# Order of a gate group's products, order of two readers of one PSUM bank, and a table lookup in 16 bits, in a two-layer encoder kernel

## The chip, the core and the metric

The kernel runs on one core of a Trainium2 chip. The metric is the time of one execution in microseconds on the device. TensorE does the matrix products (in the profile PE, its weight loads PEld), VectorE is DVE, ScalarE is ACT, GpSimd is POOL and SyncE, which issues most transfers, is SP. Each engine takes its instructions strictly in the order in which the program issues them, and waits on semaphores of the others.

## What is computed

A trunk of two layers on 256 tokens of width 1024. Each layer is an attention mixer and a PEER feed-forward part, and the change lies in the second:

```
def chunk(xc):
    q = (xc @ w_query).reshape(PEER_CHUNK, PEER_HEADS, 2, half)
    s = jnp.einsum('thpk,pnk->thpn', q, sub_keys)
    sv, si = lax.top_k(s, PEER_TOPK)
    cand = (sv[:, :, 0, :, None] + sv[:, :, 1, None, :]).reshape(...)
    cidx = (si[:, :, 0, :, None] * PEER_N_KEYS + si[:, :, 1, None, :]).reshape(...)
    top_s, sel = lax.top_k(cand, PEER_TOPK)
    eidx = jnp.take_along_axis(cidx, sel, axis=-1)
    g = jax.nn.softmax(top_s, axis=-1)
    u = expert_down[eidx]
    vv = expert_up[eidx]
    act = jax.nn.gelu(jnp.einsum('td,thkd->thk', xc, u), approximate=False)
    return jnp.einsum('thk,thkd->td', (g * act), vv)
```

For each token, 8 heads choose 16 of 128 x 128 experts each. Expert number is 128 i + j.

## The kernel before

The kernel does not gather the experts of `expert_down`. It multiplies all 16384 of them with all tokens, takes the gelu, and multiplies by a dense table of gates, which is zero where a token did not choose an expert. All products on TensorE take operands split in two (`wh`, `wl`, lines 189 and 192: ScalarE rounds the loaded tile, VectorE subtracts), so three products stand for one.

In one layer the stages of the feed-forward part follow each other so:

1. **Scores and choice** (lines 913 to 950): `score_lane`, `topk_lane`. VectorE finds the 16 best of each half and the 16 best sums.
2. **Numbers of the experts** (`index_lane`, lines 952 to 1003). A choice `sel` is a place in a 16 x 16 table. For its high and low four bits in turn, line 974 compares with 0 to 15 (2048 elements a partition), line 977 multiplies with the key numbers `sif`, and line 979 sums over the 16.
3. **Downs** (lines 1302 to 1304): 128 units a layer, each 24 products of 128x256, with two units to one PSUM bank `acc`. `gelu_lane` (lines 1234 to 1256) then has ScalarE take the gelu into `act`.
4. **Gate groups** (`gate_group`, lines 1011 to 1066), which run between the downs: 32 groups of 8 tokens for each of two halves of i, 64 a layer. For a group VectorE builds one-hot tables: `ej` of j, `ei` of i, and `ag`, which is `ei` times the gate, in two parts (high part `ag[:, 0]`, rest `ag[:, 1]`). ScalarE scales `ej` to `el` (line 1022). For each token t TensorE issues three small products: a count (`ei` with `ej`, line 1041), high gates (`ag[:, 0]` with `ej`) and low gates (`ag[:, 1]` with `el`, both line 1045). The result is a bank `b` of 8 tokens by 64 values of i.
5. **Where gate and gelu meet.** For an i whose gelu is there already (the first `g` of the 64), VectorE multiplies `act` by the gates from the bank (line 1059); for the others ScalarE copies the gates into `act` (line 1062), and `gelu_lane` multiplies later: it takes the gelu of tokens that have gates in place (line 1244), writes the gelu of the others to `act` (line 1249) and has VectorE multiply (line 1252). Where both engines read one bank, the second in program order waits for the first.
6. **Ups** (line 1336): the experts that any token chose, ranked, sent and read back, are multiplied by their gates, in products of 128x512.

What sets the order is a planner at build time (`Lanes`, from line 55). The main line emits TensorE's units; every side job is a generator, a lane, that asks for an engine with an estimated cost (`vcost`, `scost`) and is let in by a clock for each engine. The estimates decide between which units of the downs a group falls. Once emitted, the order is fixed, also that between engines. Four buffers of `wh` and `wl` let the splits run ahead, and two sets of one-hot tables and two banks let two groups overlap.

Of the kernel before, what the change touches and what calls it, by code (L numbers as in the profile page):

```python
# [12 lines left out]
F16 = mybir.dt.float16  # L13
# [42 lines left out]
def vcost(n):  # L56
    return 0.1 + n * 0.00105
# [157 lines left out]
def encoder_kernel(ctx, tc, x_in, wts, downs, ups, gains, gate_bias, qk_norm, rpb, sink, skeys, consts, sums, out,  # L215
                   depth=DEPTH):
    nc = tc.nc
# [79 lines left out]
    iota2 = cpool.tile([128, 128, 2], F16, name="iota2")  # L297
    tiny = cpool.tile([128, 2], F32, name="tiny")
# [16 lines left out]
    iota16 = cst[:, C_I16:C_I16 + 16]  # L315
# [146 lines left out]
    for l in range(depth):  # L462
# [5 lines left out]
        if l == 0:  # L468
# [23 lines left out]
            nc.vector.tensor_copy(iota2, cst[:, C_IOTA:C_IOTA + 128][:, :, None].to_broadcast([128, 128, 2]))  # L492
            acc_first = first_half(u, "T1")
# [371 lines left out]
        def area(off, n, u32=False):  # L865
            return (afu if u32 else afl)[:, A0 + off:A0 + off + n]
# [88 lines left out]
        def index_lane():  # L955
            yield from lane_need(["top"])
            for ch in range(2):
                w = lambda k: area(M2 + k * 128, 128).rearrange("p (h k) -> p h k", k=16)
                wu = lambda k: area(M2 + k * 128, 128, True).rearrange("p (h k) -> p h k", k=16)
                sif = area(M2 + 8 * 128, 256).rearrange("p (h q k) -> p h q k", q=2, k=16)  # L960
# [8 lines left out]
                nc.vector.tensor_copy(w(2), wu(1))  # L969
                nc.vector.tensor_copy(w(3), wu(7))  # L970
                for q in range(2):
                    eq = area(11264, 2048).rearrange("p (h k a) -> p h k a", h=8, a=16)
                    yield ("v", vcost(2048))
                    nc.vector.tensor_tensor(eq, w(2 + q)[:, :, :, None].to_broadcast([128, 8, 16, 16]),
                                            iota16[:, None, None, :].to_broadcast([128, 8, 16, 16]), op=OP.is_equal)
                    yield ("v", vcost(2048))
                    nc.vector.tensor_mul(eq, eq, sif[:, :, q, None, :].to_broadcast([128, 8, 16, 16]))
                    yield ("v", vcost(2048))
                    nc.vector.tensor_reduce(w(4 + q), eq, axis=AX.X, op=OP.add)
# [30 lines left out]
        def gate_group(r, n, o):  # L1010
# [29 lines left out]
            for t in range(8):  # L1040
                nc.tensor.matmul(cnts[r][:, half * w:(half + 1) * w], ej[:, t // 2, :, t % 2],
                                 ei[:, t // 2, i0 - p0:i0 - p0 + w, t % 2], start=counted[r] == 0 and t == 0,
                                 stop=counted[r] == NG - 1 and t == 7, skip_group_check=True)
                for k, e in enumerate((ej, el)):
                    nc.tensor.matmul(b[:, t * 64:(t + 1) * 64], e[:, t // 2, :, t % 2],
                                     ag[:, k, t // 2, :, t % 2], start=k == 0, stop=k == 1)
# [8 lines left out]
            g = min(max(2 * gelus[0] - p0, 0), 64)  # L1055
            if g:
                t = lanes.use("v", vcost(8 * g) - 0.35)
                a = act[:, p0:p0 + g, half, t0:t0 + 8]
                nc.vector.tensor_mul(a, a, bv[:, 0:g])
            if g < 64:  # L1060
                t = max(t, lanes.use("s", scost(8 * (64 - g)), lanes.cur - 0.3))
                nc.scalar.activation(act[:, p0 + g:p0 + 64, half, t0:t0 + 8], bv[:, g:64], AF.Copy)
# [172 lines left out]
        def gelu_lane(b, acc):  # L1235
# [9 lines left out]
            for c in range(2):  # L1245
                g0 = min(max(g - 128 * c, 0), 128)
                a, ac = act[:, 2 * b:2 * b + 2, c], av[:, :, 128 * c:128 * c + 128]
                if g0 < 128:
                    nc.scalar.activation(a[:, :, g0:128], ac[:, :, g0:128], AF.Gelu)  # L1249
                if g0:  # L1250
                    t = max(t, lanes.use("v", vcost(2 * g0), lanes.cur))
                    nc.vector.tensor_mul(a[:, :, 0:g0], a[:, :, 0:g0], ac[:, :, 0:g0])
# [255 lines left out]
```

## Time and profile before

| | |
|---|---|
| runs | 1885.28, 1888.07, 1889.13 us (median 1888.07) |
| profiled execution, its time | 1889.17 us |
| its span, first to last instruction | 1887.4 us |
| granted TensorE clock | 0.992 |
| PE busy | 1846.0 us, 98% |
| DVE busy | 1493.7 us, 79% |
| ACT busy | 1075.3 us, 57% |
| POOL busy | 423.9 us, 22% |

A matmul's busy time in the profile reaches to the end of its pipeline: a 128x256 product is shown as 282 ns, while the next one starts 120 ns later. So a busy PE can still lose time, and what it loses is read from the distances between starts. In the windows view a row gives the stretch, its length, then for each engine the busy time and in brackets the number of instructions, then granted clock, DMA share and GB/s. In the timeline a row gives start, duration, engine, line and operation, and in square brackets the idle time ahead of it with what ended it.

### The profile page before, as it was taken

How to read it: one execution, taken by the hardware profiler on the slowest of the kernel's cores; microseconds unless marked ns; L12 is line 12 of the kernel's file. 1: busy time of each engine (PE TensorE's matmuls, PEld its weight loads, DVE VectorE, ACT ScalarE, POOL GpSimd, SP SyncE). 2: the span in 40 equal slices, each digit the busy share in tenths (PEclk: the TensorE clock that was granted, in tenths of full speed). 3: DMA queues.
4: the chain of work that ended last, by engine and by line, in shares of the span. 5: the costliest groups of instructions: out<-in, count | busy, mean ns of one | idle time of the engine just before them, and what ended most of it. 6: DMA issues, size and time to landing. Idle time of an engine off the chain costs nothing. (4 is left out here: it accounts for less than half of the span.)

```text
span 1887.4 us, 37955 instructions
## 1 busy us (share of the span) xinstructions
PE 1846.0 (98%) x14826; PEld 1672.6 (89%) x14826; DVE 1493.7 (79%) x3017; ACT 1075.3 (57%) x1710; POOL 423.9 (22%) x374
## 2 busy tenths in 40 slices
PE   8999999999999999999899999999999999999998
PEld 7889899999999977888778989999999999778886
DVE  6976899888887797756689778999788877976565
ACT  4665544556556565645646654455566565666454
POOL 0000000000027456744200000000000374567341
PEclk8999999999999999999999999999999999999999
DMA  7435456554457688997464354555444587889873
GB/s 255 158 101 171 155 163 190 177 166 157 152 162 233 215 272 278 312 285 227 167 219 137 111 174 146 179 188 179 156 158 147 176 234 224 260 284 323 261 229 121
DMA packets 125139, 372.98 MB, mean 198 GB/s; under 512 B 16528, under 2 KB 38672, under 8 KB 124944
## 3 DMA queue, kind: packets, MB, share of 16 engines
q1 hardware_dynamic: 91440, 256.93, 44.2%
q0 software_dynamic: 33504, 113.47, 17.4%
q8 instruction: 120, 1.97, 0.4%
q14 instruction: 75, 0.61, 0.1%
HBM read 342.87 MB, written 27.47 MB: 196 GB/s over the span
## 5 line engine op out<-in xcount | busy, mean ns | idle before, releaser
L192 DVE TENSOR_TENSOR wl<-raw,wh 128x1024 fp32r<-128x1024 f32 x478 | 580.0, 1221 | 200.2 <-ACT wh L189 196.7
L189 ACT ACTIVATE wh<-raw 128x1024 fp32r<-128x1024 f32 x478 | 504.3, 1058 | 254.4 <-PE bank L1336 76.3
L1302 PE MATMUL bank<-TT,wh 128*128 128x256 f32 x2048 | 587.0, 287 | 0.0
L1303 PE MATMUL bank<-TT,wh 128*128 128x256 f32 x2048 | 577.2, 282 | 0.0
L1304 PE MATMUL bank<-TT,wl 128*128 128x256 f32 x2048 | 577.1, 282 | 0.0
L1336 PE MATMUL bank<-wh,TT 128*128 128x512 f32 x1416 | 397.9, 400 | 8.3 <-PEq L1351 5.9
L1302 PEld LDWEIGHTS bank<-TT,wh 128*128 128x128 f32 x2048 | 386.2, 189 | 0.3
L1303 PEld LDWEIGHTS bank<-TT,wh 128*128 128x128 f32 x2048 | 386.0, 188 | 0.0
L1304 PEld LDWEIGHTS bank<-TT,wl 128*128 128x128 f32 x2048 | 385.0, 188 | 0.0
L1336 PEld LDWEIGHTS bank<-wh,TT 128*128 128x128 f32 x1416 | 266.0, 189 | 75.0 <-issue 6.7
L1152 POOL DMA_INDIRECT rows<-act,rank x200 | 220.4, 1102 | 374.0 <-DVE miss L1124 313.6
L192 DVE TENSOR_TENSOR wl<-act,wh 128x1024 fp32r<-128x1024 f32 x132 | 161.4, 1224 | 93.1 <-ACT wh L189 87.9
L1336 PE MATMUL bank<-wl,TT 128*128 128x512 f32 x708 | 225.5, 398 | 0.0
L189 ACT ACTIVATE wh<-act 128x1024 fp32r<-128x1024 f32 x132 | 139.7, 1060 | 120.0 <-PE bank L1336 113.0
L870 POOL IOTA act<- 128x128 uint32 x4 | 1.8, 438 | 805.3 <-PE bank L355 417.5
L1249 ACT ACTIVATE act<-bank 128x256 f32<-128x256 f32 (+7 forms) x240 | 79.8, 369 | 173.1 <-PE bank L1304 121.5
L1336 PEld LDWEIGHTS bank<-wl,TT 128*128 128x128 f32 x708 | 134.1, 189 | 32.7
L1022 ACT ACTIVATE el<-ej 128x1024 f16<-128x1024 f16 x128 | 133.2, 1050 | 19.9 <-DVE ej L1019 19.3
L1211 POOL DMA_INDIRECT act<-in_ups_dram,act x96 | 117.3, 1222 | 101.4 <-DVE TT L1229 88.0
L435 PE MATMUL bank<-TT,wh 128*128 128x256 f32 x448 | 129.6, 289 | 1.5 <-ACT raw_ka L563 1.0
L437 PE MATMUL bank<-TT,wh 128*128 128x256 f32 x448 | 126.4, 282 | 0.0
L438 PE MATMUL bank<-TT,wl 128*128 128x256 f32 x448 | 126.3, 282 | 0.0
(252 smaller groups left out, 2969.9 us busy)
## 6 DMA issues: line engine op xcount, KB each, us to landing
raw<-in_downs_dram SPq DMA_DIRECT2D x256, 512.0 KB, 3.7
raw<-in_wts_dram SPq DMA_DIRECT2D x132, 512.0 KB, 3.9
act<-in_ups_dram SPq DMA_DIRECT2D x36, 512.0 KB, 5.9
act<-rows SPq DMA_DIRECT2D x82, 129.0 KB, 4.3
raw<-in_ups_dram SPq DMA_DIRECT2D x20, 512.0 KB, 5.7
act<-rows SPq DMA_DIRECT2D x84, 64.5 KB, 4.4
rows<-act,rank POOLq DMA_INDIRECT x200, 6.0
Sq<-in_rpb_dram SPq DMA_DIRECT2D x2, 876.0 KB
```

The costliest lines, as they stand in the source:

```text
L189: self.nc.scalar.activation(h, r, AF.Copy)
L192: self.splits.append(self.nc.vector.tensor_sub(lo, r, h.bitcast(F32)).ins.name)
L435: nc.tensor.matmul(o, wh, rh, start=first and i == 0 and pc == 0, stop=False, skip_group_check=True)
L437: nc.tensor.matmul(o, wh, rl, start=False, stop=False, skip_group_check=True)
L438: nc.tensor.matmul(o, wl, rh, start=False, stop=last and i == len(kcs) - 1 and pc == 1, skip_group_check=True)
L1022: nc.scalar.activation(el, ej, AF.Copy, scale=LOW)
L1152: snd = nc.gpsimd.indirect_dma_start(byrank[r], bass.IndirectOffsetOnAxis(ap=rank[:, i:i + 1], axis=0), afl[:, i * ROW:(i + 1) * ROW], None)
L1211: nc.gpsimd.indirect_dma_start(w, None, ups_rows, bass.IndirectOffsetOnAxis(ap=num, axis=0), element_offset=l * 16384 * D)
L1302: nc.tensor.matmul(o, lh, TT[:, :, 0, kc, :], start=kc == 0, stop=False)
L1303: nc.tensor.matmul(o, lh, TT[:, :, 1, kc, :], start=False, stop=False)
L1304: nc.tensor.matmul(o, ll, TT[:, :, 0, kc, :], start=False, stop=kc == 7)
L1336: nc.tensor.matmul(oacc[ch][hf], a, r[:, hf * 512:(hf + 1) * 512], start=first[hf] and a is lh and r is h, stop=last and a is ll)
```

## The change

It has four edits, and the planner lays out the whole order anew with them.

- **The group's products.** All counts and high gates of the 8 tokens come first, then the 8 low gates. The flag that starts a sum is now set once for the bank.
- **Two readers of a bank.** In `gate_group` ScalarE's copy of the late i is emitted ahead of VectorE's multiplication; in `gelu_lane` ScalarE writes the gelu for both halves first, and VectorE multiplies behind.
- **The lookup.** The table of 0 to 15, the numbers and the compared bits are float16 (the numbers are under 128). The sum over 16 is four halvings by additions.
- **The planner's figures** for these steps follow.

```
+    i16 = cpool.tile([128, 8, 2], F16, name="i16")
...
+            nc.vector.tensor_copy(i16.rearrange("p a s -> p (a s)"), cst[:, C_I16:C_I16 + 16])
...
-                nc.vector.tensor_copy(w(2), wu(1))
-                nc.vector.tensor_copy(w(3), wu(7))
+                for k in range(2):
+                    nc.vector.tensor_copy(wh(2 + k), area(M2 + (1, 7)[k] * 128, 128, True)[:, :, None].to_broadcast(
+                        [128, 128, 2]))
...
-                    yield ("v", vcost(2048))
-                    nc.vector.tensor_tensor(eq, w(2 + q)[:, :, :, None].to_broadcast([128, 8, 16, 16]),
-                                            iota16[:, None, None, :].to_broadcast([128, 8, 16, 16]), op=OP.is_equal)
-                    yield ("v", vcost(2048))
-                    nc.vector.tensor_mul(eq, eq, sif[:, :, q, None, :].to_broadcast([128, 8, 16, 16]))
-                    yield ("v", vcost(2048))
-                    nc.vector.tensor_reduce(w(4 + q), eq, axis=AX.X, op=OP.add)
+                    yield ("v", vcost(1024) + 0.3)
+                    nc.vector.tensor_tensor(eq, wh(2 + q)[:, :, None, :].to_broadcast([128, 128, 8, 2]),
+                                            i16[:, None, :, :].to_broadcast([128, 128, 8, 2]), op=OP.is_equal)
+                    yield ("v", vcost(1024))
+                    nc.vector.tensor_mul(e4, e4, sif[:, :, q, None, :].to_broadcast([128, 8, 16, 16]))
+                    for m in (8, 4, 2, 1):
+                        yield ("v", vcost((64 if m > 1 else 128) * m))
+                        nc.vector.tensor_add(w(4 + q)[:, :, :, None] if m == 1 else e4[:, :, :, 0:m], e4[:, :, :, 0:m],
+                                             e4[:, :, :, m:2 * m])
...
-                for k, e in enumerate((ej, el)):
-                    nc.tensor.matmul(b[:, t * 64:(t + 1) * 64], e[:, t // 2, :, t % 2],
-                                     ag[:, k, t // 2, :, t % 2], start=k == 0, stop=k == 1)
+                nc.tensor.matmul(b[:, t * 64:(t + 1) * 64], ej[:, t // 2, :, t % 2],
+                                 ag[:, 0, t // 2, :, t % 2], start=t == 0, stop=False, skip_group_check=True)
+            for t in range(8):
+                nc.tensor.matmul(b[:, t * 64:(t + 1) * 64], el[:, t // 2, :, t % 2],
+                                 ag[:, 1, t // 2, :, t % 2], start=False, stop=t == 7, skip_group_check=True)
...
+            if g < 64:
+                t = lanes.use("s", scost(8 * (64 - g)), lanes.cur - 0.5)
+                nc.scalar.activation(act[:, p0 + g:p0 + 64, half, t0:t0 + 8], bv[:, g:64], AF.Copy)
             if g:
-                t = lanes.use("v", vcost(8 * g) - 0.35)
+                t = lanes.use("v", vcost(8 * g) - 0.35, t if g < 64 else 0.0)
                 a = act[:, p0:p0 + g, half, t0:t0 + 8]
                 nc.vector.tensor_mul(a, a, bv[:, 0:g])
-            if g < 64:
-                t = max(t, lanes.use("s", scost(8 * (64 - g)), lanes.cur - 0.3))
-                nc.scalar.activation(act[:, p0 + g:p0 + 64, half, t0:t0 + 8], bv[:, g:64], AF.Copy)
...
             for c in range(2):
-                g0 = min(max(g - 128 * c, 0), 128)
-                a, ac = act[:, 2 * b:2 * b + 2, c], av[:, :, 128 * c:128 * c + 128]
+                g0 = max(g - 128 * c, 0)
                 if g0 < 128:
-                    nc.scalar.activation(a[:, :, g0:128], ac[:, :, g0:128], AF.Gelu)
-                if g0:
-                    t = max(t, lanes.use("v", vcost(2 * g0), lanes.cur))
-                    nc.vector.tensor_mul(a[:, :, 0:g0], a[:, :, 0:g0], ac[:, :, 0:g0])
+                    nc.scalar.activation(act[:, 2 * b:2 * b + 2, c, g0:128], av[:, :, 128 * c + g0:128 * c + 128],
+                                         AF.Gelu)
+            if g:
+                t = lanes.use("v", vcost(2 * g), t)
+                for c in range(1 + (g > 128)):
+                    a = act[:, 2 * b:2 * b + 2, c, 0:min(g - 128 * c, 128)]
+                    nc.vector.tensor_mul(a, a, av[:, :, 128 * c:min(g, 128 * c + 128)])
```

What this does to the fixed order is seen at two places. The first is TensorE's queue at the start of a gate group late in the first layer's downs (`ej1`, `el1`, `ag1` are the group's one-hot tables, `bank4` its gates, `bank7` the counts). Before:

```order
L1041 LDWEIGHTS ej1_2241 [waits DVE_49]
L1041 MATMUL bank7_7004<-ei1_2245,ej1_2241 128x36 [waits DVE_49]
L1045 LDWEIGHTS ej1_2241 [waits DVE_49]
L1045 MATMUL bank4_8745<-ag1_2247,ej1_2241 128x64 [waits PE_49]
L1045 LDWEIGHTS el1_2243 [waits Activation_49]
L1045 MATMUL bank4_8745<-ag1_2247,el1_2243 128x64 [waits DVE_49]
```

And the corresponding group now; between the fourth and the fifth row stand seven more pairs of a count and a high-gates product, which wait for nothing:

```order
L1048 LDWEIGHTS ej1_2243 [waits DVE_49]
L1048 MATMUL bank7_6901<-ei1_2247,ej1_2243 128x36 [waits DVE_49]
L1051 LDWEIGHTS ej1_2243 [waits DVE_49]
L1051 MATMUL bank4_8861<-ag1_2249,ej1_2243 128x64 [waits Activation_49]
...
L1054 LDWEIGHTS el1_2245 [waits Activation_49]
L1054 MATMUL bank4_8861<-ag1_2249,el1_2245 128x64 [waits DVE_49]
```

The waits for `el` and for the second `ag` moved from the second product into `bank4` to the ninth.

The second place is the pair that reads the same two banks, on ScalarE and on VectorE. ScalarE before (`wh` is the split of a unit, line 1062 the copy of late gates, lines 1244 and 1249 the gelu of `bank1`):

```order
L189 ACTIVATE wh_8814<-raw_8611 128x1024 [waits DMAHW5_49]
L1022 ACTIVATE el0_2242<-ej0_2240 128x1024
L1062 ACTIVATE act_2237<-bank4_8745 128x4x8 [waits DVE_49]
L1244 ACTIVATE bank1_8821<-bank1_8821 128x2x184 [waits PE_49]
L1249 ACTIVATE act_2237<-bank1_8821 128x2x72 [waits DVE_49]
```

ScalarE now:

```order
L189 ACTIVATE wh_8904<-raw_8677 128x1024 [waits DMAHW5_49]
L1067 ACTIVATE act_2239<-bank4_8861 128x4x8 [waits PE_49]
L1029 ACTIVATE el0_2244<-ej0_2242 128x1024 [waits DVE_49]
L1253 ACTIVATE bank1_8912<-bank1_8912 128x2x200 [waits PE_49]
L1257 ACTIVATE act_2239<-bank1_8912 128x2x56 [waits Activation_49]
```

VectorE before, for the same banks:

```order
L192 TENSOR_TENSOR wl_8816<-raw_8611,wh_8814 128x1024 [waits DMAHW5_49,Activation_49]
L1059 TENSOR_TENSOR act_2237<-act_2237,bank4_8745 128x60x8 [waits PE_49]
L1024 TENSOR_TENSOR ei0_2244<-iota2_71,ijT_2238 128x512
L1028 TENSOR_TENSOR ag0_2246<-ei0_2244,gT_2239 128x512 [waits DVE_49]
L1028 TENSOR_TENSOR ag0_2246<-ei0_2244,gT_2239 128x512
L1019 TENSOR_TENSOR ej1_2241<-iota2_71,ijT_2238 128x1024
L1252 TENSOR_TENSOR act_2237<-act_2237,bank1_8821 128x2x128 [waits Activation_49]
L1252 TENSOR_TENSOR act_2237<-act_2237,bank1_8821 128x2x56 [waits Activation_49]
```

VectorE now:

```order
L192 TENSOR_TENSOR wl_8907<-raw_8677,wh_8904 128x1024 [waits DMAHW5_49,Activation_49]
L1071 TENSOR_TENSOR act_2239<-act_2239,bank4_8861 128x60x8 [waits Activation_49]
L1031 TENSOR_TENSOR ei0_2246<-iota2_71,ijT_2240 128x512
L1035 TENSOR_TENSOR ag0_2248<-ei0_2246,gT_2241 128x512 [waits DVE_49]
L1035 TENSOR_TENSOR ag0_2248<-ei0_2246,gT_2241 128x512
L1026 TENSOR_TENSOR ej1_2243<-iota2_71,ijT_2240 128x1024
L1263 TENSOR_TENSOR act_2239<-act_2239,bank1_8912 128x2x128 [waits PE_49,Activation_49]
L1263 TENSOR_TENSOR act_2239<-act_2239,bank1_8912 128x2x72
```

VectorE's sequence is the same; its first reading waits for ScalarE where it waited for TensorE, and ScalarE's two waits for VectorE are gone.

In the order as a whole the first gate group of a layer stands after 46.75 units of the downs, where it stood after 52.25; the last group of the first half after 87.75, where it was 91.75. Six groups of a layer stand behind the last unit (two of them straight behind it, four among the ups), where it was eight (two, and six). The lines of `act` and of the bank keep their work, and the number of products is the same.

More of the change, by code (lines that the diff above doesn't have):

```diff
@@ L314, in encoder_kernel @@
     ident = cst[:, C_ID:C_ID + 128]
-    iota16 = cst[:, C_I16:C_I16 + 16]
     ups_rows = ups.rearrange("l i j d -> (l i j) d")
@@ L959, in index_lane @@
                 wu = lambda k: area(M2 + k * 128, 128, True).rearrange("p (h k) -> p h k", k=16)
-                sif = area(M2 + 8 * 128, 256).rearrange("p (h q k) -> p h q k", q=2, k=16)
+                sif = area(M2 + 8 * 128, 128).bitcast(F16).rearrange("p (h q k) -> p h q k", q=2, k=16)
+                wh = lambda k: area(M2 + k * 128, 128).bitcast(F16).rearrange("p (n s) -> p n s", s=2)
                 yield ("v", 0.6)
@@ L968, in index_lane @@
                 nc.vector.tensor_scalar(wu(7), sel[ch], 15, None, op0=OP.bitwise_and)
-                nc.vector.tensor_copy(w(2), wu(1))
-                nc.vector.tensor_copy(w(3), wu(7))
+                for k in range(2):
+                    nc.vector.tensor_copy(wh(2 + k), area(M2 + (1, 7)[k] * 128, 128, True)[:, :, None].to_broadcast(
+                        [128, 128, 2]))
                 for q in range(2):
-                    eq = area(11264, 2048).rearrange("p (h k a) -> p h k a", h=8, a=16)
-                    yield ("v", vcost(2048))
-                    nc.vector.tensor_tensor(eq, w(2 + q)[:, :, :, None].to_broadcast([128, 8, 16, 16]),
-                                            iota16[:, None, None, :].to_broadcast([128, 8, 16, 16]), op=OP.is_equal)
-                    yield ("v", vcost(2048))
-                    nc.vector.tensor_mul(eq, eq, sif[:, :, q, None, :].to_broadcast([128, 8, 16, 16]))
-                    yield ("v", vcost(2048))
-                    nc.vector.tensor_reduce(w(4 + q), eq, axis=AX.X, op=OP.add)
+                    eq = area(11264, 1024).bitcast(F16).rearrange("p (n a s) -> p n a s", a=8, s=2)
+                    e4 = area(11264, 1024).bitcast(F16).rearrange("p (h k a) -> p h k a", h=8, a=16)
+                    yield ("v", vcost(1024) + 0.3)
[7 more added lines that the diff above has]
+                                             e4[:, :, :, m:2 * m])
                 sm = area(M2 + 7 * 128, 8)
```

## Prediction

> **What bounds the kernel now.** The page comes first: TensorE (PE) covers the span.
>
> ```profile
> PE 1846.0 (98%) x14826; PEld 1672.6 (89%) x14826; DVE 1493.7 (79%) x3017; ACT 1075.3 (57%) x1710; POOL 423.9 (22%) x374
> ```
>
> Since a matmul's row reaches to its modelled end, 98% hides lost time; what was lost is read from counts. The windows view of stretches that hold only downs and gate groups, then of the first ups, then a longer stretch around the end of the downs:
>
> ```profile
> 300.00:386.00 86.00, 86.00 (x719) 86.00 (x718) 79.88 (x149) 46.02 (x68) 0.00 (x0) 1.00 0.57 183
> 455.00:541.00 86.00, 86.00 (x1047) 85.03 (x1047) 75.97 (x126) 52.21 (x70) 0.00 (x0) 1.00 0.49 153
> 400.00:455.00 55.00, 54.11 (x651) 52.88 (x651) 42.88 (x75) 32.88 (x58) 0.00 (x0) 1.00 0.45 144
> 590.00:676.00 86.00, 81.00 (x924) 77.82 (x923) 66.85 (x121) 49.31 (x84) 51.71 (x47) 1.00 0.76 230
> 1338.00:1393.00 55.00, 53.98 (x644) 52.70 (x641) 42.85 (x74) 32.74 (x57) 0.00 (x0) 1.00 0.45 145
> 1527.00:1613.00 86.00, 81.84 (x931) 78.70 (x930) 67.23 (x122) 48.55 (x84) 50.94 (x47) 1.00 0.77 229
> 679.00:684.00 5.00, 5.00 (x17) 3.95 (x14) 3.87 (x7) 2.72 (x6) 1.87 (x2) 0.54 0.97 385
> 1617.00:1622.00 5.00, 5.00 (x19) 4.05 (x20) 4.03 (x8) 2.75 (x5) 1.87 (x2) 0.81 0.90 334
> 1700.00:1750.00 50.00, 50.00 (x215) 40.22 (x214) 33.75 (x46) 30.45 (x46) 37.21 (x33) 1.00 0.94 320
> 590.00:684.00 94.00, 87.44 (x961) 82.92 (x960) 73.20 (x132) 52.98 (x91) 55.85 (x51) 0.96 0.78 241
> ```
>
> The lines view gives the counts of line 1041, one third of the gate products, in 455:541, 400:455, 590:676, 1338:1393 and 1527:1613:
>
> ```profile
> L1041 PE MATMUL bank<-ei,ej 128*128 128x64 f16 x153 | 16.2, 194 | 0.0
> L1041 PE MATMUL bank<-ei,ej 128*128 128x64 f16 x96 | 10.4, 194 | 0.1
> L1041 PE MATMUL bank<-ei,ej 128*128 128x36 f16 x128 | 13.8, 181 | 0.1
> L1041 PE MATMUL bank<-ei,ej 128*128 128x64 f16 x94 | 10.3, 194 | 0.1
> L1041 PE MATMUL bank<-ei,ej 128*128 128x36 f16 x128 | 13.9, 181 | 0.1
> ```
>
> In 300:386 there are only downs: 86/719 = 0.1196 us each. In 455:541 no group is held up: 1047 - 459 = 588 downs take 70.3, and the rest, 15.7/459, is 0.0342 us for a gate product. By these prices 590:676 needs 540 x 0.1196 + 384 x 0.0342 = 77.7 of its 86 us: 8.3 lost. Likewise 1527:1613 loses 86 - 78.5 = 7.5, 400:455 loses 1.7 and 1338:1393 loses 2.1. The timeline shows where: inside the groups, and between two of them at the end of the downs. The first two rows are one group, the next two the first and last of 44 low-gates products that came late (0.04 us or more; 13.0 us in all, 0.44 at most); then comes the end of the downs:
>
> ```profile
> 601.59 0.19 PE L1045 MATMUL bank<-ag,ej 128*128 128x64 f16 x1
> 601.99 0.20 PE L1045 MATMUL bank<-ag,el 128*128 128x64 f16 x1 [0.21 <-ACT el L1022]
> 421.05 0.20 PE L1045 MATMUL bank<-ag,el 128*128 128x64 f16 x1
> 1644.04 0.19 PE L1045 MATMUL bank<-ag,el 128*128 128x64 f16 x1
> 673.71 0.67 DVE L1059 TENSOR_TENSOR act<-act,bank 128x496 f32<-128x496 f32 x1
> 674.29 0.68 DVE L1019 TENSOR_TENSOR ej<-iota,ijT 128x1024 f16<-128x1024 f16 x1
> 674.41 0.19 ACT L1062 ACTIVATE act<-bank 128x16 f32<-128x16 f32 x1 [2.06 <-DVE act L1059]
> 674.45 0.19 PE L1045 MATMUL bank<-ag,el 128*128 128x64 f16 x1
> 674.49 1.05 ACT L189 ACTIVATE wh<-raw 128x1024 fp32r<-128x1024 f32 x1
> 675.57 1.23 DVE L192 TENSOR_TENSOR wl<-raw,wh 128x1024 fp32r<-128x1024 f32 x1 [0.60 <-ACT wh L189]
> 676.72 0.42 DVE L1024 TENSOR_TENSOR ei<-iota,ijT 128x512 f16<-128x512 f16 x1
> 677.19 0.19 PE L1041 MATMUL bank<-ei,ej 128*128 128x36 f16 x1 [2.54 <-DVE ei L1024]
> 677.65 0.23 PE L1045 MATMUL bank<-ag,ej 128*128 128x64 f16 x1 [0.27 <-DVE ag L1028]
> 677.98 0.21 PE L1045 MATMUL bank<-ag,el 128*128 128x64 f16 x1
> ```
>
> Here PE stands from 674.48 to 677.19, then 0.43 and 0.30 more: 3.4 us, of which 1.5 lie before 676 and are counted already. The other layer ends its downs with the same pair of groups (the waits below show two such stalls of 5.1 us together). Not counted yet: 4.6 us over both. Behind it the granted clock is down: 17 and 19 ups products in 5 us, where 1700:1750 has 0.2326 us each, so 1.05 and 0.58 us are lost. I estimate 1.5 us for groups among the ups (1644.04 is one). All that gate groups cost PE in stalls is 8.3 + 7.5 + 1.7 + 2.1 + 4.6 + 1.6 + 1.5 = 27.3 us.
>
> Next the waits, in 590:684 for the two engines that feed the groups, and for the whole span:
>
> ```profile
> DVE wl L192 <- ACT wh L189: 16.1, 18, 1.4
> DVE act L1252 <- ACT act L1249: 2.7, 7, 0.4
> ACT act L1062 <- DVE act L1059: 26.1, 15, 2.6
> ACT act L1249 <- DVE act L1252: 13.7, 13, 1.6
> ACT act L1062 <- DVE act L1059: 96.1, 62, 3.0
> PE bank L1041 <- DVE ei L1024: 5.1, 2, 2.6
> ```
>
> In this stretch VectorE waits for ScalarE (16.1 + 2.7 us) and never for PE, so it is late by itself. ScalarE has only 53 us of work in 94, but stands 39.8 us behind VectorE's readings of shared banks, and the splits queued behind come late for VectorE. The rows from 673.71 to 677.19 are one such round: reading, wait of 2.06, split, wait of 0.60, `ei`, PE.
>
> **The change part by part.**
>
> *Low gates last.* Nothing is added: 24 products, 24 weight loads. Between the first product into the bank and the first that needs `el` and the second `ag` stand 14 more products; in an unstalled group they start 0.03 us apart, so they cover 0.41 us. The 44 late ones (0.44 at most) vanish but for crumbs: 13.0 becomes about 0.5. Outside the dense stretches that is paid at once; within, it counts only if VectorE comes earlier, or PE waits the same time at `ei` or the first `ag`. Bounds: 0 and 13.0.
>
> *ScalarE reads first.* In 590:684 the 39.8 us of ScalarE's waits go. VectorE's multiplication gets a wait for ScalarE's copy; behind it on VectorE stand the next group's `ei`, `ag` and `ej`, for which PE waits. The nearest price of that copy is 0.28 us:
>
> ```profile
> L1062 ACT ACTIVATE act<-bank 128x80 f32<-128x80 f32 (+16 forms) x70 | 19.4, 279 | 96.1 <-DVE act L1059 96.1
> ```
>
> That is 0 where VectorE is late, as in the dense stretches, and 15 x 0.28 = 4.2 us a layer where it is not. I take 0: in the order VectorE has a split of 1.2 us ahead of this reading, time enough for the copy. VectorE's 73.2 us of work in 590:684 then stand against PE's need of 94 - 8.3 - 1.9 (the rest of the pair) - 1.0 (clock) = 82.8. If its 19 us of waits fall to 8, it needs 81, and PE sets the pace again; the margin is thin, so single groups will still wait. Of 15.8 us lost in the two dense stretches (13.6 without what belongs to the pair at the end), 8.6 are low gates (counted likewise) and 5.0 `ei` and first `ag`. I leave 0.5 and 2.0: gain 11.1. Of 3.8 us in the early stretches 2.8 are low gates (counted like the 44), and I leave 1.0: gain 2.8. Among the ups: gain 0.8.
>
> *The pair at the end.* It is still there, with the same work on VectorE between the two groups (a reading, `ej`, a split, `ei`): about 2.8 us of rows, and 0.60 of wait that goes. PE gives it 1.25 units of downs (30 x 0.1196 = 3.6 us) and a group of 0.8, counted from the group before; VectorE on time makes that, VectorE late by 2 us doesn't. Of 6.8 us of stall and 1.6 us at a low clock I leave 2: gain 6.4. [...]
>
> *The lookup.* Before, and the nearest 16-bit rows:
>
> ```profile
> L974 DVE TENSOR_TENSOR act<-act,cst 128x2048 f32<-128x2048 f32 x8 | 18.3, 2284 | 0.0
> L1028 DVE TENSOR_TENSOR ag<-ei,gT 128x512 f16<-128x512 f16 x256 | 97.7, 423 | 4.4
> L1019 DVE TENSOR_TENSOR ej<-iota,ijT 128x1024 f16<-128x1024 f16 x128 | 87.4, 685 | 0.0
> ```
>
> Compare, multiply and sum go over the same 2048 elements, 2.28 us each by this row, 6.85 us a lookup. In 16 bits the rows for 512 and 1024 give 0.51 ns an element and 0.16 fixed: 1.21 + 1.21, and the additions 0.69 + 0.42 + 0.29 + 0.29; together 4.1. Four lookups a layer save 11 us of VectorE, or lose 1.4 if 16 bits bring nothing (2.28 + 2.28 + 2.6). PE gains nothing at once: it runs without a gap in 300:386, where buffered splits cover the lookups. Where the cover is gone, a late group costs what VectorE is late. What it buys is room: groups start 5.5 units earlier (by the order, 5.5 x 24 x 0.1196 = 15.8 us), so VectorE has more downs over which to spread them. I count that as part of its margin above. The one cast for the 0-to-15 table lies in the start-up; by the 0.16 us fixed it costs 0 to 0.2, taken as 0.2.
>
> The sum: 11.1 + 2.8 + 0.8 + 6.4 - 0.2 = 20.9 us. The profiled execution took 1889.2, so 1868.3 in its own terms; it lies 1.1 us above the median of the runs, which gives 1867.
>
> **The rivals.**
>
> *VectorE keeps the pace.* Its waits may change their name and not their length, since it has 73 us of work in 82.8 and two partners in order. For it: PE's early arrival gives VectorE nothing. Against it: ScalarE's 39.8 us. Then only the early stretches, the ups and some of the 2.7 us a layer at line 1252 are won: 2.8 + 0.8 + 2 = about 6 us, 1882.
>
> *The wait turned round.* VectorE now stands behind ScalarE at each pair. If ScalarE has a split or `el` (1.05 us) still to do when the bank is ready, the reading is late by 1.05 + 0.28 = 1.3 us: 15 pairs make 20 us a layer, on top of 73.2 and the 16.1 that stay, 109 in a stretch of 94, so the kernel loses 15 us a layer instead of gaining: 1889 + 30, less some 15 for the gains elsewhere (2.8 + 0.8 + 6.4) and the lead VectorE has when the stretch begins, = 1904. It decides once ScalarE's backlog is over 1 us; 39.8 us of idling speak against that. [...]
>
> *The groups come too early.* If 16 bits bring nothing on VectorE, groups placed 15.8 us earlier find no tables: up to 12 us a layer at the first groups, less what the buffers cover; with the gains above, 1867 + 24 = 1891. Rows 1019 and 1028 speak against it.
>
> *Nothing to see.* New waits eat what the old ones leave: 1888.
>
> **How the numbers follow.** Forecast 0.72, VectorE keeps the pace 0.15, turned round 0.05, too early 0.03, nothing 0.05. A measurement of this kernel can tell about 0.2%, 3.8 us, from no change. The forecast and most of the second case (0.13) are faster: 0.85. Same: 0.02 + 0.05 = 0.07. Slower: 0.08. All 27.3 us and some of VectorE's waits elsewhere would give 1858; the second case's 1882 with a little on it is the upper end: 1858 to 1883.
>
> **What would show it.** Right: in the dense stretch before the last unit the low-gates rows start 0.03 us behind the high-gates rows; ScalarE's waits for VectorE at the copy and the gelu are gone; PE's count in 86 us there rises from 924 to about 1000; the granted clock stays at 1.00 behind the downs. Wrong: VectorE waiting for the copy for over 10 us a layer, PE's waits for `ei` or `ag` grown by what the low gates lost, or a stall at the first group of a layer.

## The result, and the profile after

| | time, median us | runs | ratio to before (95%) | predicted |
|---|---|---|---|---|
| before | 1886.76 | 1885.28 to 1889.13 | | |
| after | 1838.02 | 1836.43 to 1839.21 | 0.974 (0.9723 to 0.9757) | 1867 (1858 to 1883) |

The gain is 48.7 us, where 20.9 were forecast: more than twice as much, and outside the range. The profiled execution of after took 1839.15 us, its span 1837.3. TensorE's lines on the page of after:

```profile
PE 1808.9 (98%) x14826; PEld 1646.7 (90%) x14826; DVE 1475.7 (80%) x3054; ACT 1081.3 (59%) x1726; POOL 437.0 (24%) x374
PEclk9999999999999999999999999999999999999999
```

The same 14826 products are busy for 37 us less. The windows view of after, first for a stretch of downs alone, then for the last 86 us of the first layer's downs (the last down now starts at 655.9, in before at 673.1, so the prediction's 590:676 has become 570:656), then straight behind them, then for ups:

```profile
250.00:340.00 90.00, 90.00 (x766) 90.00 (x766) 89.07 (x297) 46.66 (x69) 0.00 (x0) 1.00 0.62 193
570.00:656.00 86.00, 86.00 (x1027) 85.23 (x1025) 72.69 (x132) 54.83 (x91) 56.41 (x48) 1.00 0.80 244
657.00:659.00 2.00, 1.60 (x27) 1.32 (x27) 1.97 (x6) 1.59 (x4) 1.48 (x2) 1.00 0.95 375
659.00:661.00 2.00, 2.00 (x10) 1.63 (x9) 2.00 (x4) 0.12 (x1) 1.61 (x2) 1.00 1.06 375
1700.00:1750.00 50.00, 50.00 (x216) 40.30 (x215) 28.12 (x36) 24.18 (x37) 17.78 (x18) 1.00 0.85 252
```

The first of these stretches in before:

```profile
250.00:340.00 90.00, 90.00 (x754) 90.00 (x753) 87.94 (x294) 46.34 (x67) 0.00 (x0) 1.00 0.58 182
```

TensorE waits for nothing in either, no gate group stands there, the granted clock is 1.00 in both, and yet TensorE has 766 products in 90 us instead of 754. From start to start a down takes 117.8 ns on average instead of 119.9, an up 233.3 instead of 234.3. No edit alters these products. That is the part of the gain that the prediction did not have.

The part that it had is there too. VectorE's waits in 573:667 of after, which lies to the end of the downs as 590:684 did in before; those of ScalarE for VectorE at the copy and at the gelu (39.8 us in before) are no longer among ScalarE's:

```profile
DVE wl L192 <- ACT wh L189: 6.1, 12, 0.8
DVE act L1071 <- ACT act L1067: 2.9, 2, 1.7
DVE act L1263 <- ACT act L1257: 1.3, 2, 0.9
```

VectorE waits 10.3 us there instead of 18.8, and TensorE has 1027 products in 86 us instead of 924. The timeline of the last pair of groups before the end of the downs in after (line 1026 writes `ej`, 1031 `ei`, 1035 `ag`; 1048 is the count, 1051 the high, 1054 the low gates):

```profile
654.91 0.69 DVE L1026 TENSOR_TENSOR ej<-iota,ijT 128x1024 f16<-128x1024 f16 x1
655.51 1.22 DVE L192 TENSOR_TENSOR wl<-raw,wh 128x1024 fp32r<-128x1024 f32 x1
656.46 0.19 PE L1051 MATMUL bank<-ag,ej 128*128 128x64 f16 x1
656.49 0.41 PE L1054 MATMUL bank<-ag,el 128*128 128x64 f16 x8
656.65 0.42 DVE L1031 TENSOR_TENSOR ei<-iota,ijT 128x512 f16<-128x512 f16 x1
657.10 0.76 DVE L1035 TENSOR_TENSOR ag<-ei,gT 128x512 f16<-128x512 f16 x2
657.12 0.18 PE L1048 MATMUL bank<-ei,ej 128*128 128x36 f16 x1 [0.23 <-DVE ei L1031]
```

The wait of 2.54 us for `ei` has become 0.23, and the low gates start 0.03 us behind the high ones; the first high gates are still held up behind the count, as in before. For the rest of this text a gate product is called late when it starts over 0.04 us behind the usual distance from its predecessor, and its lateness is what is over that usual distance:

| late products: number, us | count (`ei`) | high gates (`ej`, first `ag`) | low gates (`el`, second `ag`) | sum us |
|---|---|---|---|---|
| before | 10, 6.8 | 30, 9.2 | 44, 13.0 | 29.0 |
| after | 2, 0.8 | 4, 1.3 | 0 | 2.1 |

So some 27 us would be the edits' and 20 us the shorter products'. The experiments ask where the 20 come from, and which edit made the 27.

### The profile page after: what moved, and what is told of

Its sections match the earlier page's. It is cut to its first block, busy times and chain, and to the rows that moved or that the text cites. A ratio compares the mean times of both kernels' runs of the same rounds, so it can differ in the third digit from the quotient of the medians.

```text
span 1837.3 us, 38009 instructions
## 1 busy us (share of the span) xinstructions
PE 1808.9 (98%) x14826; PEld 1646.7 (90%) x14826; DVE 1475.7 (80%) x3054; ACT 1081.3 (59%) x1726; POOL 437.0 (24%) x374
## 5 line engine op out<-in xcount | busy, mean ns | idle before, releaser
L1161 POOL DMA_INDIRECT rows<-act,rank x200 | 234.2, 1171 | 371.6 <-DVE miss L1133 311.3
L1257 ACT ACTIVATE act<-bank 128x256 f32<-128x256 f32 (+8 forms) x238 | 74.5, 362 | 108.3 <-PE bank L1315 106.4
```

The lines of the kernel that those rows point to most:

```text
L1161: snd = nc.gpsimd.indirect_dma_start(byrank[r], bass.IndirectOffsetOnAxis(ap=rank[:, i:i + 1], axis=0), afl[:, i * ROW:(i + 1) * ROW], None)
```

## The experiments

**Theory.** The edit of the lookup adds a tile, `i16`, of 32 bytes a partition, between `iota2` and everything that is allocated behind it. `TT` lies ahead of it and stays; `wh` and `wl` move by 32 bytes. By the sizes of the tiles between them (small ones taken as 32 bytes) `wh` stands 36768 bytes behind `TT` in before and 36800 in after, modulo 256 that is 160 and 192. Every down and every up takes one operand from `TT` and the other from `wh` or `wl`. The theory is that the distance between the two sets the price of a product. **Rivals**: that the products got shorter by something that the edits do (VectorE's lighter lookup), or that it was another chip.

The chips were not alike. Full clock but for short stretches was granted on those of e13 and e18 to e22, where the kernel before took 1886 to 1890 us, as above, at a mean granted clock of 0.990 to 0.996. On the others it took 1951 to 1963 us at 0.972 to 0.983; they come last.

### The price of a product by addresses: e13

It leaves out everything but products of the two forms, on data taken from `x`.

```python
for k in range(32):
    downs_like(0, 8 * k)        # wh, wl first at 32*k bytes; 4 units, 96 products
for k in range(1, 4):
    downs_like(8 * k, 0)        # TT moved by 32*k bytes
```

> The price of a product alone, against the addresses of its operands: this kernel leaves out everything but products of the downs' form (128x128 stationary, 256 moving columns, the same order of high and low halves, the same tile sizes, 96 in a row) and of the ups' form (512 columns, 12 in a row), on data taken from x. The stationary tiles' first address goes through all 32 places of 32 bytes in 1024 (place 3 is that of the kernel before, place 4 that of the changed kernel, place 5 that of the changed kernel with another 32 bytes); then the moving tile goes through three further places. Nothing else runs. Theory (addresses alone set the price): place 3 gives 120.0 ns, place 4 117.8, place 5 117.8 or 116.7, and the places fall into a few classes. Rival (the price depends on what other engines do in the full kernels, whose addresses moved too): all places alike.

The windows view of e13, 9 us from each of eight neighbouring places (number of products in brackets; a product is shown for some 280 ns, so two or three of them began ahead of the stretch); `wh` stands 64, 96, 128, 160, 192, 224, 0 and 32 bytes behind `TT`, modulo 256. The ninth row is a second place with 64:

```profile
218.76:227.76 9.00, 9.00 (x82) 9.00 (x81) 0.00 (x0) 0.00 (x0) 1.00 0.00 0
230.45:239.45 9.00, 9.00 (x79) 9.00 (x78) 0.00 (x0) 0.00 (x0) 1.00 0.01 2
242.50:251.50 9.00, 9.00 (x78) 9.00 (x77) 0.00 (x0) 0.00 (x0) 1.00 0.01 2
254.66:263.66 9.00, 9.00 (x77) 9.00 (x76) 0.00 (x0) 0.00 (x0) 1.00 0.01 2
266.95:275.95 9.00, 9.00 (x79) 9.00 (x78) 0.00 (x0) 0.00 (x0) 1.00 0.00 0
279.05:288.05 9.00, 9.00 (x79) 9.00 (x78) 0.00 (x0) 0.00 (x0) 1.00 0.01 2
291.14:300.14 9.00, 9.00 (x77) 9.00 (x76) 0.00 (x0) 0.00 (x0) 1.00 0.01 2
303.43:312.43 9.00, 9.00 (x78) 9.00 (x77) 0.00 (x0) 0.00 (x0) 1.00 0.01 2
121.42:130.42 9.00, 9.00 (x79) 9.00 (x78) 0.00 (x0) 0.00 (x0) 1.00 0.00 0
```

From start to start over the last 24 products of each place that is

| distance mod 256 | 64 | 96 | 128 | 160 | 192 | 224 | 0 | 32 |
|---|---|---|---|---|---|---|---|---|
| ns a product | 113.3 | 117.2 | 118.7 | 120.0 | 117.8 | 117.8 | 120.0 | 118.3 |

and the row repeats every eight places, but for 64 and 96: at 64, three of the four places ran at 113.3 and one at 117.8, at 96 they ran at 117.2 to 118.6. Moving `TT` by 32, 64 and 96 bytes instead, with `wh` at the first place, gave 118.3, 120.0 and 116.7. The first two are the scan's prices of the distances 32 and 0; the third, 224, had 117.8 at all four places of the scan, and e2 below, which stands at 224 too, shows both 117.8 and 116.7. So the distance sets the price up to a choice between two steady rhythms at some distances. The kernel before stands at 160, after at 192, where the scan has 120.0 and 117.8 and the kernels 119.9 and 117.8. The scan's products of the ups' form, twelve in a row at each place, are too few to tell the places apart (224 to 238 ns). Nothing else runs in this kernel, so the rival of other engines falls. What in the chip makes the distance count is not shown; these runs show only that it does, with a period of 256 bytes.

### The addresses alone in the kernel: e19

```diff
     iota2 = cpool.tile([128, 128, 2], F16, name="iota2")
+    pad = cpool.tile([128, 8], F32, name="pad")
```

> The kernel before with the unused 32-byte tile: the addresses alone. With full clock: 1867 to 1870 us if addresses and edits add up; 1872 to 1880 if faster products make the gate groups stall longer. With the clock held back: 0.989 to 0.993 of the kernel before, as measured.

Measured: 1873.79 us, 0.9935 (0.9918 to 0.9951): 12.5 us gained by a tile that nothing reads. The windows view of e19:

```profile
250.00:340.00 90.00, 90.00 (x766) 90.00 (x765) 89.67 (x293) 46.65 (x69) 0.00 (x0) 1.00 0.60 188
```

The products are after's. That only 12.5 of some 20 us arrive is the second case of the expectation, and its reason is there too: late gate products are 17, 8.4 us, 36, 11.2 us and 45, 14.5 us, 34.1 in all where before has 29.0. TensorE reaches the groups earlier, and VectorE does not.

### The edits alone: e18

```diff
     i16 = cpool.tile([128, 8, 2], F16, name="i16")
+    pad = cpool.tile([128, 56], F32, name="pad")
```

> The changed kernel with an unused tile of 224 bytes behind i16: with i16's 32 that moves wh and wl by 256 bytes, so that they stand 160 bytes (modulo 256) behind TT as in the kernel before. Theory (the distance modulo 256 sets the price): downs 120.0 ns apart again; the edits alone remain, 1858 us with full clock (1838 + 20), against the 1867 that the prediction had for them. Rival (any address other than that of the kernel before will do): 117.8 ns and 1838 us.

Measured: 1858.18 us, 0.9854 (0.9838 to 0.987), as the theory had it. The windows view of e18, in the stretch without gates and in the last 86 us of the first layer's downs (the last one starts at 665.9):

```profile
250.00:340.00 90.00, 90.00 (x754) 90.00 (x753) 87.81 (x299) 46.34 (x67) 0.00 (x0) 1.00 0.57 182
580.00:666.00 86.00, 86.00 (x1002) 85.18 (x998) 72.70 (x131) 53.62 (x89) 55.16 (x47) 1.00 0.79 240
```

754 products again, and 1002 in the dense stretch where before has 924, with the same 384 gate products among them: at the old price of a product this is what the prediction wrote down, "from 924 to about 1000". The late products are 2, 0.6 us and 4, 1.3 us. So the edits alone give 28.1 us and the addresses, added to them, 20.2 (1858.2 to 1838.0); without the edits the addresses give 12.5. The two lean on each other: 5.1 of the 7.7 us between the two figures are the later gate products of e19, which the edits remove; each gain is known to some 3 us.

### Which edit: e21 and e20

The planner lays out the order anew for each of these two kernels, so each shows an edit together with the order that follows from it.

e21 puts both readings back as they were (VectorE's multiplication first, then ScalarE's copy or gelu of the same bank); low gates last and the lookup stay.

```diff
-            if g < 64:
-                t = lanes.use("s", scost(8 * (64 - g)), lanes.cur - 0.5)
-                nc.scalar.activation(act[...], bv[:, g:64], AF.Copy)
             if g:
...
                 nc.vector.tensor_mul(a, a, bv[:, 0:g])
+            if g < 64:
+                t = max(t, lanes.use("s", scost(8 * (64 - g)), lanes.cur - 0.3))
+                nc.scalar.activation(act[...], bv[:, g:64], AF.Copy)
...
```

> The changed kernel with VectorE's readings of a shared bank first again. With full clock: the pair of groups at the end of the downs stalls again, ScalarE stands behind VectorE's readings, single groups wait for ei and the first ag as in the kernel before (about 16 us of waits there before, the pair's included): 8 to 18 us more than the changed kernel's 1838, so 1846 to 1856. Rival (low gates last and the lighter lookup give the time alone): under 3 us, 1838 to 1841. With the clock held back: no difference from the changed kernel can be told.

Measured: 1864.22 us, 0.9873 (0.9857 to 0.989), 26 us above after and more than the 8 to 18 that were expected. The waits of e21, ScalarE's and VectorE's in 590:684 and TensorE's in the whole span:

```profile
ACT act L1071 <- DVE act L1068: 24.4, 14, 2.6
ACT act L1258 <- DVE act L1261: 12.5, 12, 1.8
DVE wl L192 <- ACT wh L189: 13.1, 18, 1.4
PE bank L1048 <- DVE ei L1031: 8.1, 14, 2.0
PE bank L1051 <- DVE ag L1035: 7.0, 26, 0.3
```

All as in the kernel before, with one difference: the low gates are hardly late (12, 1.0 us), but the counts (22, 11.5 us) and the high gates (38, 13.7 us) are late more often than in before. What the low gates no longer waited for, TensorE waited for at the first two tables: this is the prediction's rival "VectorE keeps the pace", true of low gates last without the readers' edit.

The pair at the end of the downs is back as well, and so is the clock. Windows of e21 around it, 1 us each (TensorE stands until 671.12):

```profile
670.00:671.00 1.00, 0.00 (x0) 0.00 (x0) 1.00 (x2) 0.42 (x1) 0.80 (x1) 1.00 1.22 332
671.00:672.00 1.00, 0.59 (x11) 0.42 (x11) 0.97 (x4) 0.00 (x0) 0.69 (x2) 0.74 0.75 258
672.00:673.00 1.00, 1.00 (x19) 1.00 (x17) 1.00 (x2) 0.52 (x2) 0.78 (x1) 0.50 1.02 344
673.00:674.00 1.00, 1.00 (x3) 0.79 (x3) 0.62 (x3) 0.51 (x3) 0.91 (x1) 0.50 0.95 356
```

Behind an idle time of 2.04 us stands half the clock here; in after, with 0.23 us, the clock stays at 1.00. The length of the idle time alone doesn't decide, though: in before one of 3.65 us (924.18 to 927.83) cost no clock, while the clock fell to 0.50 in one of 2.54 us (674.65 to 677.19). In before and after, the start and the end of the program left out, every stretch of half clock begins on a grid of 3.41 us (in before at 676.81, 946.46, 1130.78, 1615.47 and 1864.64, in after at 902.48 and 1103.87), behind a step in which TensorE stood for 0.49 to 0.91 of the time. Of the six steps with 0.49 to 0.55 three were followed by it, of those with less none; the 3.65 us lie in two steps with 0.53 and 0.54. What sets the grid is not shown.

e20 takes the other edit out of the changed kernel:

```diff
-                nc.tensor.matmul(b[...], ej[...], ag[:, 0, ...], start=t == 0, stop=False, skip_group_check=True)
-            for t in range(8):
-                nc.tensor.matmul(b[...], el[...], ag[:, 1, ...], start=False, stop=t == 7, skip_group_check=True)
+                for k, e in enumerate((ej, el)):
+                    nc.tensor.matmul(b[...], e[...], ag[:, k, ...], start=k == 0, stop=k == 1)
```

> The changed kernel with high and low gates side by side again for each t. With full clock: 4 to 13 us more than the changed kernel's 1838 if el and the second ag are still the last tables to be written; under 3 us if the readers' order and the lighter lookup bring all tables in time, as the traces with the clock held back suggest (two late low-gates products there that VectorE or ScalarE ended, where the kernel before has 44). With the clock held back: no difference.

Measured: 1838.24 us, 0.9741 (0.9722 to 0.976), the time of after. Late are 2, 4 and 4 products, 3.3 us. With the readers in the new order the tables are in time, whether the low gates come last or not.

| late products: number, us | count | high gates | low gates | sum us | time us |
|---|---|---|---|---|---|
| e19: no edit, new addresses | 17, 8.4 | 36, 11.2 | 45, 14.5 | 34.1 | 1873.8 |
| e21: low gates last, lookup | 22, 11.5 | 38, 13.7 | 12, 1.0 | 26.2 | 1864.2 |
| e20: readers, lookup | 2, 0.8 | 4, 1.3 | 4, 1.2 | 3.3 | 1838.2 |
| after: all three | 2, 0.8 | 4, 1.3 | 0 | 2.1 | 1838.0 |

### A better distance: e22

```diff
     i16 = cpool.tile([128, 8, 2], F16, name="i16")
+    pad = cpool.tile([128, 32], F32, name="pad")
```

> The changed kernel with wh and wl 64 bytes (modulo 256) behind TT. With full clock: ups 229.0 ns apart instead of 233.3, 2124 of them, 9 us; downs between 117.8 (nothing) and 113.3 (28 us), by the mixture of its first trace 116.7, 6 us; a few us for the projections: 1815 to 1829. Rival (gate groups stall longer with faster products, as they did with the addresses alone): 1829 to 1838. With the clock held back: 0.985 as before.

Measured: 1822.99 us, 0.9657 (0.964 to 0.9675), 15 us below after and the fastest of all. Ups stand 229.0 ns apart, downs change between 113.3 and 117.8 along a layer (mean 115.8), which would be some 12 + 9 us; a part of it is not paid. The windows view of e22, for ups and for the first downs of a layer, then these downs in after, then a wait of TensorE in e22 (line 1316 is the third product of a down):

```profile
1700.00:1750.00 50.00, 50.00 (x221) 41.00 (x220) 28.45 (x37) 25.03 (x38) 12.14 (x13) 1.00 0.76 232
244.00:340.00 96.00, 94.26 (x821) 93.67 (x821) 95.90 (x317) 50.55 (x73) 0.00 (x0) 1.00 0.58 187
244.00:340.00 96.00, 96.00 (x818) 96.00 (x817) 95.07 (x315) 50.43 (x73) 0.00 (x0) 1.00 0.60 187
PE bank L1316 <- DVE wl L192: 3.5, 6, 0.8
```

In the first downs of a layer, where VectorE also chooses the experts, it is busy for 95.9 of 96 us, and TensorE, though each product is shorter, gets through 821 products instead of 818, since it has to wait for `wl`. There VectorE has become the limit. That explains part of what is not paid; the rest is open.

### On chips that hold the clock back

Twelve runs fell on three chips where the same programs took longer.

| kernel | ratio to before (95%) |
|---|---|
| *before: 1963.4 us* | |
| e1: before, 32-byte tile | 0.9892 (0.9838 to 0.9947) |
| e2: after, another 32-byte tile | 0.9817 (0.9766 to 0.9868) |
| e3: before, low gates last alone | 0.9983 (0.9963 to 1.0003) |
| e4: before, readers alone | 0.9997 (0.9975 to 1.0018) |
| *before: 1960.9 us* | |
| e12: after | 0.9932 (0.9908 to 0.9956) |
| e6: after without the lookup | 0.994 (0.9902 to 0.9978) |
| e9: after without low gates last | 0.9932 (0.9903 to 0.9961) |
| e10: after without the readers | 0.9861 (0.9836 to 0.9885) |
| *before: 1951.1 us* | |
| e14: as e22 | 0.9845 (0.9772 to 0.9918) |
| e15: as e1 | 0.9933 (0.9892 to 0.9975) |
| e16: as e9 | 0.985 (0.9811 to 0.9888) |
| e17: as e10 | 0.9826 (0.9779 to 0.9873) |

What was expected of the first four, of e12 and of e6 (for e9, e10 and e14 to e17 see the kernels of the same make above):

> The kernel before with one thing added: an unused tile of 32 bytes a partition behind iota2, where the changed kernel has its new table i16; no instruction is added or altered. Theory (addresses): the 32 bytes move wh, wl and the other operands of the products from 32 bytes behind a 64-byte boundary onto one, and that alone shortened the products. The downs then stand 117.8 ns apart instead of 119.9 (300:386 counts about 730 products instead of 719), the ups 233.3 instead of 234.3, and the time falls by about 20 us, to some 1867; the stalls of the gate groups stay as before, 29 us. Rival (something else in the change, or another chip, shortened them): 119.9 ns as before and 1887 us.

> The changed kernel with another unused tile of 32 bytes behind i16, so that wh, wl and the gate tables lie again as they did before; all instructions as in the changed kernel. Theory (addresses): downs 119.9 ns apart again, the gate groups as free of stalls as in the changed kernel, the time about 1857 (1838 + 20). Rival (the shorter products come from the edits themselves, for instance from VectorE's lighter traffic in the lookup): 117.8 ns and 1838 us.

> The kernel before with the first edit alone, the eight low-gates products last in their group; addresses as before, so 119.9 ns a down. Theory (the prediction's): the 13.0 us of late low-gates products vanish, but in the dense stretches before the last downs VectorE is late anyway and part of the time comes back as waits for ei and the first ag: 4 to 9 us gained, about 1880. Rival (low gates are the last wait everywhere): all 13 gained, 1874. Rival (VectorE keeps the pace): 3 to 4 us, 1883, with the waits for ei and ag grown by as much as those for el shrank.

> The kernel before with the second edit alone, ScalarE's reading of a shared bank ahead of VectorE's, at the gate copy and at the gelu; addresses as before. Theory (the prediction's): ScalarE's 39.8 us of waits at the end of each layer's downs go, splits and tables come earlier, the low-gates stalls that ScalarE's el ended (5 us) go, the pair at the end of the downs and the low clock behind it (6.8 + 1.6 us) go too: some 8 to 14 us gained, 1873 to 1879. Rival (the wait is only turned round, VectorE standing where ScalarE stood): no gain, 1886 or more. Rival (room for VectorE comes only with the lighter lookup): under 4 us.

> The changed kernel itself once more, as the measure for the three kernels run beside it, each of which lacks one of the edits and keeps the changed kernel's addresses. On a chip that grants the clock as it did in the first comparison: 0.974 of the kernel before. On one that holds the clock back under load (as the chip of the last four kernels did, where the kernel before took 1963 us) every theory expects less: stalls that go are given back as clock; 0.98.

> The changed kernel with the lookup in 32 bits as before (a spare 32-byte tile in the place of i16 keeps the addresses). Theory (the prediction's: the lookup pays nothing itself, but 11 us of VectorE's time a layer are part of its margin in the dense stretches): the groups start 5.5 units later and single groups wait again for ei and ag, 2 to 6 us more than the changed kernel, 1840 to 1844. Rival (the lookup is what lets VectorE keep up): most of the 15 us of the dense stretches come back, 1850 or more. Rival (no part at all): 1838.

The windows view of e12, the changed kernel, on such a chip:

```profile
250.00:340.00 90.00, 90.00 (x767) 90.00 (x766) 89.08 (x297) 46.59 (x69) 0.00 (x0) 1.00 0.60 189
540.00:560.00 20.00, 10.05 (x63) 8.20 (x62) 5.05 (x9) 3.81 (x9) 9.66 (x10) 0.67 0.36 123
1500.00:1600.00 100.00, 78.71 (x796) 74.89 (x796) 55.03 (x101) 43.79 (x75) 58.90 (x53) 0.85 0.56 176
```

Up to some 540 us it runs as on the first chip. Then, from the later gate groups of each layer on, TensorE stands in pieces of up to 3.6 us for no wait that the profile shows ("issue"), half of 540:560, and the granted clock is below 1. In e12 these pieces come to 61 us, where after has 0.4. In all TensorE is idle for 71 us longer than in after, and for 48 us longer its products run (1857.2 instead of 1808.9 us busy, at a mean clock of 0.967 instead of 0.997); together that is the 119 us between the profiled executions. Most of the gain is lost on that chip: 0.993 instead of 0.974, where 0.98 was expected. The reason given for that, that stalls which go are given back as clock, was the author's estimate, and it is not shown: the mean clock was 0.967 to 0.970 in e12 and 0.973 to 0.981 in before on that chip, but on the third one 0.975 to 0.980 in e16 and 0.972 to 0.983 in before. There e16 and e17, which lack one edit each, kept 0.985 and 0.983. Even the order of the versions changes: without the readers' edit the kernel is faster than after on the chip of e12 (e10), with full clock 26 us slower (e21). Why TensorE stands there is open, as is why the versions differ, and neither e3 nor e4 could decide anything in its time. Their traces could, if only the late products are counted for which the profile names VectorE or ScalarE. Low gates last alone (e3) leaves 9 counts, 15 high gates and 1 low gate late; the readers alone (e4) leave 2, 5 and 5; e1, with neither, leaves 7, 13 and 15. That is the same picture as e21 and e20.

The price of a product did not depend on the chip. e1 has the 117.8 ns of after, which the edits can't have made there, and e3 and e4 have the 119.9 of before. e2 refuted the first form of the theory, by which `wh` had to lie on a 64-byte boundary: it lies 32 bytes off one, as in before, and its downs take 117.8 at first and 116.7 from about the 36th unit on. That led to the scan.

## Why the prediction was wrong, point by point

**The step that failed** is the price of what is not edited. The sum is one of stalls, "11.1 + 2.8 + 0.8 + 6.4 - 0.2", and its ceiling, "all 27.3 us and some of VectorE's waits elsewhere would give 1858", takes it that the more than 10,000 long products cost the same afterwards. The new tile entered the sum as its cast alone, "0 to 0.2, taken as 0.2". Its real term was its 32 bytes: 20.2 us with the edits in place (e18 against after), of which 6144 downs x 2.1 ns = 12.9 us, 1728 products of the projections (lines 435 to 438) x 1.8 = 3.1 and 2124 ups x 1.0 = 2.1 are the largest. The working could not have priced it from before's trace, where only one distance occurs, but it could have seen that the addresses move, and left the range open below. That the kernel would be faster was forecast at 0.85; but 20 of the 48.7 us have nothing to do with the forecast's reason.

**The edits' sum**: 20.9 forecast, 28.1 measured (e18: 1858.2 against 1886.3). The stalls that it named are those that went, but two terms were mis-sized. The late products of before come to 29.0 us, where the prediction counted 25.7 (27.3 without the 1.6 of the low clock). And the remainders were too large: 0.5 + 2.0 us in the dense stretches, 1.0 in the early ones, 0.7 among the ups and 2.0 in the pair by the prediction, together 6.2; in e18 1.5 are left in the pairs of both layers, 0.4 among the ups and nothing else, together 1.9. The 3.3 and the 4.3 us make up the difference to 28.1, within the 3 us to which it is known.

**Low gates last.** "The 44 late ones vanish" is right, and wrong as a reason for the time: without this edit after is no slower (e20), and without the readers' edit what the low gates no longer waited for came back at `ei` and `ag` (e21). The 8.6 and 2.8 us that the sum put on the low gates belong to tables that came late, by VectorE's doing at 30 of the 44 and by ScalarE's at 14; the low gates were only the last to show it.

**ScalarE reads first.** "I take 0" for the new wait in the dense stretch: 2.9 us in 573:667. VectorE's waits "fall to 8": 10.3. So PE sets the pace, as said, but without this edit the changed kernel takes 26 us more (e21), of the 36 that all the edits gain at these addresses (e19 to after), which is far more than the part that the sum gave it. The warning sign that was named, "VectorE waiting for the copy for over 10 us a layer", came and meant nothing. VectorE's waits in the whole span of after:

```profile
DVE act L1071 <- ACT act L1067: 24.5, 20, 2.0
DVE act L1263 <- ACT act L1257: 10.0, 14, 1.0
```

12 us a layer, most of it outside the dense stretches, where only two gate products are late, by 0.19 us each. The sign should have named the stretch.

**The pair at the end**: 2 us left of 8.4 by the forecast. In after the count is late by 0.39 us and the first high gates by 0.43, at the end of either layer's downs, 1.6 us in all, with no low clock behind. This term was right.

**The lookup.** The groups of after on VectorE (compare, multiply, additions):

```profile
L979 DVE TENSOR_TENSOR act<-act,i 128x2048 f16<-128x2048 f16 x8 | 9.8, 1220 | 0.0
L982 DVE TENSOR_TENSOR act<-act 128x2048 f16<-128x2048 f16 x8 | 9.8, 1222 | 0.1
L985 DVE TENSOR_TENSOR act<-act 128x1024 f16<-128x1024 f16 (+3 forms) x32 | 16.7, 521 | 0.8
```

1.22 + 1.22 + 4 x 0.52 = 4.5 us a lookup, where 4.1 was forecast. What the lookup adds to the time by itself stays open: it was taken out only on a chip that held the clock back (e6, 0.994 beside 0.9932). The waits of TensorE for the groups' tables in e6 speak for a small part of its own, as the prediction's margin had it:

```profile
PE bank L1042 <- DVE ei L1025: 2.7, 5, 1.1
PE bank L1045 <- DVE ag L1029: 1.1, 4, 0.3
```

In e12, with the lookup, on the same chip, no such wait shows. With low gates last the lookup brought about 10 us (e19 to e21).

**The rivals.** "VectorE keeps the pace" holds without the readers' edit; "the wait turned round", "too early" and "nothing to see" did not come.

## What to carry to other kernels

Before pricing an edit, look at which tiles it adds, resizes or reorders: whatever is allocated behind moves, and a product whose operands lie at another distance can cost up to 6% more or less (113.3 to 120.0 ns in e13) without one instruction changed. Where TensorE bounds the kernel, scan that distance in a kernel of products alone, pad to the best, and look for the engine that becomes the limit then. And where several products wait in turn for one late engine, removing the last wait only shows the one before it; ask what makes that engine late.

## What the runs showed of the hardware

- The rate of fp32r products of 256 columns depends on the distance of the two operands in a partition, with a period of 256 bytes in steps of 32: 113.3 to 120.0 ns (e13). The ups of 512 columns went from 234.3 (distance 160, before) to 233.3 (192, after) and 229.0 (64, e22).
- The same code at the same addresses can run in two rhythms, 113.3 and 117.8 ns at distance 64 (e13), and change between them within a layer (e22).
- Half the clock came behind a TensorE idle for 2.04 us (e21, at 671) and not behind one idle for 3.65 us (before, at 924); it begins on a grid of 3.41 us, behind steps that were idle for 0.49 to 0.91 of the time (before and after).
- On three chips the kernel before took 1951 to 1963 us at a mean granted clock of 0.972 to 0.983. On one of them TensorE stood for no wait that the profile shows, 61 us in all, and its clock fell from some 540 us on, to 0.67 in 540:560 (e12); what made it so is not shown. There a gain of 2.6% shrank to 0.7% (e12), and the order of versions was another (e10, 0.9861).
